# Moving weight scales, sums of squares and four weight sums from GpSimd to VectorE in a hybrid attention layer

## The chip, the cores and the metric

The kernel runs on one core of a Trainium2 chip. The core has a matrix engine (TensorE, PE in the profile), three engines for elementwise work (VectorE or DVE, ScalarE or ACT, GpSimd or POOL) and a sequencer (SyncE or SP) that here only issues DMAs. Each engine works through its own queue of instructions in order and waits on semaphores for the others; all DMAs share 16 DMA engines. Matmuls read SBUF and write PSUM banks of 512 float32 per partition. The metric is the device time of one execution in microseconds. A profile of one execution shows when each instruction ran and what it waited for.

## The reference

One encoder layer over 1024 tokens of width 1024, all in float32: an RMS norm, one input projection whose columns feed two kinds of attention (a sliding window and a 2-D neighbourhood), an output projection with a residual, a second RMS norm, a gated MLP of width 2816 whose gate passes a convolution of width 3, and a final RMS norm.

```python
hn = rmsnorm(h, norm_mix[l])
proj = jnp.einsum('bsd,de->bse', hn, w_in[l])
...                                   # o_a, o_b: the two attentions
mix = jnp.concatenate([rmsnorm(o_a, norm_a[l]), rmsnorm(o_b, norm_b[l])], axis=-1)
h = h + jnp.einsum('bse,ed->bsd', mix, w_out[l])
hn = rmsnorm(h, norm_ffn[l])
g = jnp.einsum('bsd,df->bsf', hn, w_gate); u = jnp.einsum('bsd,df->bsf', hn, w_up)
g = depthwise_conv3(g, conv_w) + conv_b
h = h + jnp.einsum('bsf,fd->bsd', jax.nn.silu(g) * u, w_down)
return rmsnorm(h, norm_final)
```

## The kernel before, in words

Tokens lie on the free axis in two halves of 512 (`h` = 0 and 1); features lie on the 128 partitions, so the width 1024 is 8 tiles `d` and the MLP width 2816 is 22 tiles `f`, called units. From the output projection on, float32 products are made of three 16-bit products: a weight and an operand are each split into an upper half (ScalarE copies to float16, `hi`, `whi`) and a lower half (VectorE subtracts, `lo`, `wlo`), and PE multiplies upper by upper, upper by lower and lower by upper. So every weight tile costs ScalarE one pass and VectorE one pass (L1062 for `wp`, L1089 for `wo`, L1141 for the rest) before PE can use it.

Weights are scaled into the range of float16 by a power of two. For a unit, ScalarE squares its gate and up weights with a running sum per row (`head_scan` L1054 into `head_rows` for the first four units, `scan_rows` L1154 into `w_rows` for the others, 24 more scans into `d_rows` for `w_down`). `settle_scales` (L1015) adds the gate and up sums (`wv`, L1021), and `measure` (L1006) takes their maximum over the partitions, by transposing on PE (`wm`, L1001) and reducing on VectorE (`m`, L1003), and then makes the scale: GpSimd clamps and multiplies (L1010) and raises to the power -1/2 (L1011), VectorE masks out all but the exponent (L240). Then come the inverse (`back`, L1024 and L1025) and the scaled taps of the convolution (`taps`, L1028). `settle_scales` runs twice for two of the first four units, during the output projection, and for four units at a time later on; `joint` (L1405 on) uses `measure` for the operands of the last product.

The stage around the change is the second part of the output projection (L1234 on). For each half `h` and each `d`, PE makes 12 matmuls into a bank `pj`; `settle_out` (L1184) adds the result to the residual on VectorE (`h<-pj`, L1188; the order lists call the eight tiles `h_4132`, `h_4249`, `h_4368`, `h_4494`, `h_4625`, `h_4703`, `h_4775`, `h_4777`), spills it by a DMA issued from ScalarE's queue, squares it on ScalarE (`s`, L1192) and adds the square to a running sum (`s<-s,s`, L1194): on GpSimd for the first half, on VectorE for the second. When a half is done, PE transposes the sum (`st`, L220), VectorE reduces it (`v`, L222 and L223), GpSimd raises it to -1/2 (L224), PE widens it over the partitions (`sw`, L255), VectorE multiplies `h` by it (`normed`, L1199), and `operands` splits it (`hg`, ScalarE L1172 and VectorE L1173).

In between, the first four units' weights are prepared. The MLP's products are formed by a scheme with seven products instead of eight, which takes sums and differences of weight blocks. `pure` splits two raw blocks of each unit (`wp<-rw`), and `head_weights` (L1204) forms `s1`, the sum of two blocks of the up weights (L1209, on GpSimd; tile `ws`), and then `s2`, `s4`, `s3` by subtractions on VectorE (L1201). The squares `s` and the sums `ws` share one set of six buffers of 512 columns, of which the four units' sums hold four.

PE's order is that of the program. On the other engines a scheduler sets it before the kernel runs: it takes instructions by priority and by its own estimate of when their inputs are ready; `high_priority` lifts some ahead. That order is then fixed, so an instruction that waits holds up all behind it on its engine. DMAs that load weights stand in SP's queue; a load into a buffer waits there until the buffer is free, and there are two buffers for scans.

Of the kernel before, what the change touches and what calls it, by code (L numbers as in the profile page):

```python
# [16 lines left out]
I32 = mybir.dt.int32  # L17
AF = mybir.ActivationFunctionType
ALU = mybir.AluOpType
# [36 lines left out]
C_END = 128  # L56
V_TOP, P_TOP, TINY = 2.0 ** 14, 2.0 ** 15, 1e-30
X_TOP, W_TOP, FAINT = 2.0 ** 7, 2.0 ** 13, 1e-24

K_ID, K_MA, K_MB, K_SCALE, K_END = 0, 128, 512, 896, 897  # L60


def hybrid_layer(tc, xT, w_in, w_out, w_gate, w_up, w_down, small, sink, rpb, consts, rope, out):
    nc = tc.nc
    with ExitStack() as ctx:
# [40 lines left out]
        minus_half = cpool.tile([128, 4], F32, name="minus_half")  # L106
# [120 lines left out]
        def inverse_narrow(sqs, dim, tag, n=4):  # L227

            ps = bank("ss", tag)
            for i, sq in enumerate(sqs):  # L230
                for c in range(n):
                    nc.tensor.matmul(ps[:, c:c + 1], sq[:, c * 128:(c + 1) * 128], ones[:, 0:1], start=c == 0 and i == 0,
                                     stop=i == len(sqs) - 1, skip_group_check=True)
            v = cpool.tile([128, 4], F32, name="v4", tag="v4", bufs=4)
            nc.scalar.activation(v[:, 0:n], ps[:, 0:n], AF.Sqrt, bias=eps, scale=float(D) / dim)
            nc.vector.reciprocal(v[:, 0:n], v[:, 0:n])
            return v

        def exponent(x):
            nc.vector.tensor_scalar(x.bitcast(I32), x.bitcast(I32), 0x7F800000, None, op0=ALU.bitwise_and)  # L240
# [478 lines left out]
        t = quarters(big("f", "mix"))  # L719
# [174 lines left out]
        for g in range(2):  # L894
            for b in range(NB):
                q, t, w = unit_window(g, b)
# [52 lines left out]
        for u in range(len(flat)):  # L949
            q, t, need, kind, _ = flat[u]  # L950
# [55 lines left out]
        def measure(v, tag):  # L1006

            with tc.high_priority(offset=500):
                s = spread_max(v, tag)
                nc.gpsimd.tensor_scalar(s, s, FAINT, W_TOP ** -2, op0=ALU.max, op1=ALU.mult)  # L1010
                nc.gpsimd.tensor_tensor(s, s, minus_half[:, 0:s.shape[1]], op=ALU.pow)  # L1011
                exponent(s)
            return s

        def settle_scales(i, n, tag):  # L1015

            fs = FO[i:i + n]
            n = len(fs)
            rows = (w_rows if i >= HEAD else head_rows)[:, 2 * i:2 * i + 2 * n].rearrange("p (n s) -> p n s", s=2)
            v = small("wv", 4)[:, 0:n]  # L1020
            nc.gpsimd.tensor_tensor(v, rows[:, :, 0], rows[:, :, 1], op=ALU.add)  # L1021
            s = measure(v, tag)
            back = little(4, "back", "backs", 4)[:, 0:n]
            nc.vector.reciprocal(back, s)  # L1024
            nc.gpsimd.tensor_tensor(back, back, unit_back.to_broadcast([128, n]), op=ALU.mult)  # L1025
            for j, f in enumerate(fs):
                taps = little(3, "taps", "taps", 12)
                nc.gpsimd.tensor_scalar(taps, par[:, C_CW + 3 * f:C_CW + 3 * f + 3], back[:, j:j + 1], 1.0, op0=ALU.mult, op1=ALU.mult)  # L1028
                scale_of[f], back_of[f], taps_of[f] = s[:, j:j + 1], back[:, j:j + 1], taps
# [67 lines left out]
        with behind("flip", "xr"):  # L1097
            for d in range(0, WO_EARLY, 2):
                t = big("wr", "op")[:, :].rearrange("p (d j c) -> p d j c", d=2, c=128)
# [9 lines left out]
        for h in range(2):  # L1109
            wide = widen(vb2[h], "pt")  # L1110
            for i in range(4):
                x = mix[4 + i][:, tsl(h)]
# [69 lines left out]
        late, total = [], [None, None]  # L1182
        at = lambda k, h: h1[k][:, tsl(h)]

        def settle_out():
            d, h, ps = late.pop(0)
            with tc.high_priority(offset=300):
                nc.vector.scalar_tensor_tensor(at(d, h), ps, wo_back, at(d, h), op0=ALU.mult, op1=ALU.add)  # L1188
            nc.scalar.dma_start(spilled[d][:, tsl(h)], at(d, h))
            s2 = half("s2")  # L1190
            with tc.high_priority(offset=300):
                nc.scalar.activation(s2, at(d, h), AF.Square)  # L1192
                if total[h] is not None:
                    (nc.gpsimd if d < (8, 0)[h] else nc.vector).tensor_tensor(s2, s2, total[h], op=ALU.add)  # L1194
            total[h] = s2

        def normed(h, wide, ds):
# [7 lines left out]
        def head_weights(i, name):  # L1205
            f, t = FO[i], wsum[i]
            g, u = head_raw[f]
            if name == "s1":
                nc.gpsimd.tensor_tensor(t, u[:, 0:4], u[:, 4:8], op=ALU.add)  # L1209
            elif name == "s2":  # L1210
                sub(t, t, g[:, 0:4])
            elif name == "s4":
                sub(t, g[:, 4:8], t)
            elif name == "s3":
                sub(t, g[:, 0:4], u[:, 0:4])
            else:
                t = u[:, 4:8]
            if name == "s1":
                if i % 2 == 0:
                    s1_places.extend(parts_places())  # L1220
                W[f, name] = two_parts(s1_places.pop(0), t, scale_of[f])
            else:
                W[f, name] = split_w(t, 4, scale_of[f])
# [4 lines left out]
        for d in range(WO_EARLY, KT):  # L1228
            if d % 2 == 0:
                t = fpool.tile([128, KT, 128], F32, name="raw", tag="raw", bufs=3)  # L1230
            wo_raw[d] = t[:, 4 * (d % 2):4 * (d % 2) + 4]
            nc.sync.dma_start(wo_raw[d], w_out[d, :, 4:8, :])
        for h in range(2):
            for d in range(KT):  # L1234
# [6 lines left out]
                if h == 1 and d == 1:  # L1241
                    with tc.high_priority(offset=300):
                        v = inverse_power(total[0], D, "pt")
# [612 lines left out]
```

## Time and profile before

| | |
|---|---|
| median of 3 runs | 1054.0 us (1052.48 to 1055.39) |
| the profiled execution | 1052.08 us, span 1050.3 us |
| PE busy | 1012.7 us, 96% |
| DVE busy | 886.0 us, 84% |
| ACT busy | 677.2 us, 64% |
| POOL busy | 247.2 us, 24% |
| GpSimd's power L1011, ten of them | 560 to 1262 ns |
| GpSimd's sums `ws` L1209, four of them | 1282 to 1796 ns |
| GpSimd's sums `s` L1194, seven of them | 1255 to 1723 ns |

Rows of the timeline read: start in us from the span's beginning, length in us of the group, engine, line, operation, tile written <- tiles read, shape, count, and in brackets the idle time of the engine just before it and what ended that. A group's length is the time from the start of its first to the end of its last instruction; neighbours on DVE overlap a little, since the next starts before the last has ended. Rows of waits read: who waited <- for whom, us in total, times, longest. Rows of groups give the shortest, median and longest in ns, and the first and last start.

### The profile page before, as it was taken

Reading aid. Unit: us, or ns where it says so; the run is one execution under the profiler, and the core shown is the slowest. Engines: PE = TensorE matmul, PEld = TensorE weight load, DVE = VectorE, ACT = ScalarE, POOL = GpSimd, SP = SyncE. Lnnn points to the kernel's source line nnn. Section 1 sums busy time; section 2 is a strip of 40 time slices with the busy share of each in tenths; the row PEclk is TensorE's granted clock in tenths of the full one; section 3 lists DMA queues with packets and bytes.
Section 4 is the critical chain, followed back from the end, with each engine's and each line's share of the span. In section 5 each row is a group of like instructions: output and inputs, shape, how many; then the busy total and the mean of one; then the engine's idle time right before and its main releaser. Section 6 shows DMA issues by size and latency. Waiting matters only on the chain.

```text
span 1050.3 us, 15578 instructions
## 1 busy us (share of the span) xinstructions
PE 1012.7 (96%) x5026; PEld 572.2 (54%) x5026; DVE 886.0 (84%) x1720; ACT 677.2 (64%) x1243; POOL 247.2 (24%) x379
## 2 busy tenths in 40 slices
PE   9998999999999977999999999999999999999996
PEld 7776777777775533444444444444444444444446
DVE  7699998766898789999899888888888889999874
ACT  8467787768687575778687875345454657655551
POOL 2235454676875344100101001001000000000002
PEclk9999999999999998999999999999999999999998
DMA  9437574686699743654767763332333678878744
GB/s 349 146 94 150 109 141 89 143 168 132 136 184 227 255 177 120 221 175 146 251 228 249 253 228 104 111 110 101 111 109 122 207 255 305 303 251 269 248 147 161
DMA packets 144274, 191.26 MB, mean 182 GB/s; under 512 B 77376, under 2 KB 88640, under 8 KB 144192
## 3 DMA queue, kind: packets, MB, share of 16 engines
q1 hardware_dynamic: 133536, 164.51, 54.9%
q10 hardware_dynamic: 10656, 25.76, 6.4%
q8 instruction: 39, 0.64, 0.3%
q14 instruction: 43, 0.35, 0.1%
HBM read 132.81 MB, written 28.57 MB: 154 GB/s over the span
## 4 chain that ended last, share of the span: by engine, by line
PE 60%; DVE 10%; ACT 4%; DMA 3%; issue 2%; POOL 1%; ACTq 0%; DVEq 0%; POOLq 0%
PE dn L1167 6%; PE dn L1165 6%; PE dn L1166 6%; PE z L1166 4%; PE z L1167 4%; PE z L1165 4%; PE pj L179 3%; PE y L1165 3%; PE y L1167 3%; PE y L1166 3%; PE x L1165 3%; PE x L1167 3%; PE x L1166 3%; PE pj L171 2%; PE pj L173 2%
## 5 line engine op out<-in xcount | busy, mean ns | idle before, releaser
L1167 PEld LDWEIGHTS <-wlo 128*128 128x128 f16 x898 | 87.8, 98 | 101.5 <-DVE wlo L1141 0.4
L1166 PEld LDWEIGHTS <-whi 128*128 128x128 f16 x898 | 87.8, 98 | 101.2 <-issue 0.9
L1165 PEld LDWEIGHTS <-whi 128*128 128x128 f16 x898 | 88.0, 98 | 100.2
L1167 PE MATMUL dn<-xd,wlo 128*128 128x512 f16 (+1 forms) x330 | 120.4, 365 | 0.0
L1166 PE MATMUL dn<-xd,whi 128*128 128x512 f16 (+1 forms) x330 | 120.4, 365 | 0.0
L1165 PE MATMUL dn<-xd,whi 128*128 128x512 f16 (+1 forms) x330 | 120.4, 365 | 0.0
L171 PE MATMUL pj<-xgh,whi 128*128 128x512 f32 x248 | 107.3, 433 | 0.6 <-ACT whi L155 0.6
L1167 PE MATMUL z<-hg,wlo 128*128 128x512 f16 x264 | 100.1, 379 | 0.0
L1165 PE MATMUL z<-hg,whi 128*128 128x512 f16 x264 | 100.1, 379 | 0.0
L1166 PE MATMUL z<-hg,whi 128*128 128x512 f16 x264 | 100.1, 379 | 0.0
L173 PE MATMUL pj<-xgh,wlo 128*128 128x512 f32 x248 | 98.3, 396 | 1.4 <-POOL wlo L156 1.4
L458 ACT ACTIVATE p<-p,nm 128x385 f32<-128x385 f32 (+3 forms) x128 | 74.7, 584 | 38.5 <-DVE nm L454 33.8
L172 PE MATMUL pj<-xgl,whi 128*128 128x512 f32 x248 | 97.9, 395 | 0.0
L1140 ACT ACTIVATE whi<-ws,m 128x512 f16<-128x512 f32 (+1 forms) x96 | 65.6, 708 | 33.2 <-DVE ws L1288 25.4
L1141 DVE SCALAR_TENSOR_TENSOR wlo<-ws,m,whi 128x512 f16<-128x512 f32 (+1 forms) x96 | 70.1, 739 | 13.2 <-ACT whi L1140 13.1
L1154 ACT ACTIVATE scan<-scan 128x1024 f32<-128x1024 f32 (+1 forms) x60 | 61.1, 1018 | 22.3 <-DMA scan<-in_w_down_dram 12.5
L1010 POOL TENSOR_SCALAR m<-m 128x4 f32<-128x4 f32 (+2 forms) x10 | 4.0, 404 | 256.1 <-DVE m L1003 255.9
L1141 DVE SCALAR_TENSOR_TENSOR wlo<-raw,m,whi 128x512 f16<-128x512 f32 (+1 forms) x78 | 55.1, 731 | 7.4 <-ACT whi L1140 6.7
L1165 PE MATMUL y<-hg,whi 128*128 128x512 f16 x160 | 60.6, 379 | 0.7 <-DVE c L1336 0.7
L1167 PE MATMUL y<-hg,wlo 128*128 128x512 f16 x160 | 60.6, 379 | 0.0
L1166 PE MATMUL y<-hg,whi 128*128 128x512 f16 x160 | 60.6, 379 | 0.0
L1140 ACT ACTIVATE whi<-raw,m 128x512 f16<-128x512 f32 (+1 forms) x78 | 51.5, 699 | 12.0 <-DMA raw<-in_w_down_dram 10.6
(290 smaller groups left out, 2490.1 us busy)
## 6 DMA issues: line engine op xcount, KB each, us to landing
xd<-x SPq DMA_DIRECT2D x77, 256.0 KB, 5.0
raw<-in_w_down_dram SPq DMA_DIRECT2D x64, 256.0 KB, 3.9
x<-c ACTq DMA_DIRECT2D x22, 512.0 KB, 2.9
scan<-in_w_gate_dram SPq DMA_DIRECT2D x18, 512.0 KB, 3.6
scan<-in_w_up_dram SPq DMA_DIRECT2D x18, 512.0 KB, 4.5
raw<-in_w_gate_dram SPq DMA_DIRECT2D x18, 512.0 KB, 3.5
raw<-in_w_up_dram SPq DMA_DIRECT2D x18, 512.0 KB, 3.8
raw<-in_w_in_dram SPq DMA_DIRECT2D x32, 256.0 KB, 3.2
```

Of the source, the lines that this page charges most:

```text
L171: nc.tensor.matmul(ps, w[0], x[0][:, tsl(h)], start=first, stop=False)
L172: nc.tensor.matmul(ps, w[0], x[1][:, tsl(h)], start=False, stop=False)
L173: nc.tensor.matmul(ps, w[1], x[0][:, tsl(h)], start=False, stop=last)
L179: nc.tensor.matmul(ps, a, b, start=i == 0 and b is x[h][0] and a is w[0], stop=i == len(ws) - 1 and a is w[1])
L458: nc.scalar.activation(p[:, 0:e], p[:, 0:e], AF.Exp, bias=nm, scale=-1.0, accum_out=sm)
L1010: nc.gpsimd.tensor_scalar(s, s, FAINT, W_TOP ** -2, op0=ALU.max, op1=ALU.mult)
L1140: nc.scalar.activation(hi, src, AF.Copy, scale=by)
L1141: nc.vector.scalar_tensor_tensor(lo, src, by, hi, op0=ALU.mult, op1=ALU.subtract)
L1154: nc.scalar.activation(t, t, AF.Square, accum_out=dst)
L1165: nc.tensor.matmul(ps, w[0], x[0], start=first and i == 0, stop=False, skip_group_check=True)
L1166: nc.tensor.matmul(ps, w[0], x[1], start=False, stop=False, skip_group_check=True)
L1167: nc.tensor.matmul(ps, w[1], x[0], start=False, stop=last and i == len(ws) - 1, skip_group_check=True)
```

## The change

Three things are different. First, the scale of a block is found on VectorE alone (`root_scale`): the float's bits are shifted right by one and masked, inverted and masked, and the result is multiplied by a constant, so that a power of two with half the negated exponent comes out; the clamp and the power on GpSimd are gone, and so is the mask `exponent` at this place. The scale can differ from the one before by a factor of two. Second, `wv` is added on VectorE. Third, all running sums of squares of the output projection and the four sums `s1` are added on VectorE. The power L224 of the norms stays on GpSimd, as do `back` and `taps`.

```diff
+W_ROOT = W_TOP * 2.0 ** 63
...
+        def root_scale(x):
+
+            i = x.bitcast(I32)
+            nc.vector.tensor_scalar(i, i, 1, 0x3FC00000, op0=ALU.logical_shift_right, op1=ALU.bitwise_and)
+            nc.vector.tensor_scalar(i, i, 0x3FC00000, 0x7F800000, op0=ALU.bitwise_xor, op1=ALU.bitwise_and)
+            nc.vector.tensor_scalar(x, x, W_ROOT, None, op0=ALU.mult)
...
             with tc.high_priority(offset=500):
                 s = spread_max(v, tag)
-                nc.gpsimd.tensor_scalar(s, s, FAINT, W_TOP ** -2, op0=ALU.max, op1=ALU.mult)
-                nc.gpsimd.tensor_tensor(s, s, minus_half[:, 0:s.shape[1]], op=ALU.pow)
-                exponent(s)
+                root_scale(s)
             return s
...
             v = small("wv", 4)[:, 0:n]
-            nc.gpsimd.tensor_tensor(v, rows[:, :, 0], rows[:, :, 1], op=ALU.add)
+            nc.vector.tensor_tensor(v, rows[:, :, 0], rows[:, :, 1], op=ALU.add)
...
                 if total[h] is not None:
-                    (nc.gpsimd if d < (8, 0)[h] else nc.vector).tensor_tensor(s2, s2, total[h], op=ALU.add)
+                    nc.vector.tensor_tensor(s2, s2, total[h], op=ALU.add)
...
             if name == "s1":
-                nc.gpsimd.tensor_tensor(t, u[:, 0:4], u[:, 4:8], op=ALU.add)
+                nc.vector.tensor_tensor(t, u[:, 0:4], u[:, 4:8], op=ALU.add)
```

The scheduler gives new orders to VectorE, ScalarE, GpSimd and SP; PE's order is the same. The rows below have each kernel's own line numbers; those of the changed kernel are 6 to 8 higher (L1188 is L1194 now, L1062 is L1068, L1089 is L1095, L1194 is L1200, L1209 is L1215).

VectorE from the first two scales on, before:

```order
L1188 SCALAR_TENSOR_TENSOR h_4249<-pj,wo_back,h_4249 128x512
L1003 TENSOR_REDUCE m<-wm 128x2
L1089 SCALAR_TENSOR_TENSOR wo<-wr,wo_by,wo 128x512
L240 TENSOR_SCALAR m<-m 128x2
L1089 SCALAR_TENSOR_TENSOR wo<-wr,wo_by,wo 128x512 x3
L1024 RECIPROCAL back<-m 128x2
```

and now:

```order
L1027 TENSOR_TENSOR wv<-head_rows 128x2
L1194 SCALAR_TENSOR_TENSOR h_4249<-pj,wo_back,h_4249 128x512
L1011 TENSOR_REDUCE m<-wm 128x2
L1095 SCALAR_TENSOR_TENSOR wo<-wr,wo_by,wo 128x512
L243 TENSOR_SCALAR m<-m 128x2
L1095 SCALAR_TENSOR_TENSOR wo<-wr,wo_by,wo 128x512
L244 TENSOR_SCALAR m<-m 128x2
L1200 TENSOR_TENSOR s_4993<-s_4993,s_4974 128x512
L245 TENSOR_SCALAR m<-m 128x2
L1095 SCALAR_TENSOR_TENSOR wo<-wr,wo_by,wo 128x512 x2
L1194 SCALAR_TENSOR_TENSOR h_4368<-pj,wo_back,h_4368 128x512
L1030 RECIPROCAL back<-m 128x2
```

The second `wv` stands ahead of `h_4249`, and the three bit steps and an `s` addition stand between the four `wo` halves.

VectorE ahead of tiles 6 and 7 of `wo` (`wo<-raw`), before:

```order
L240 TENSOR_SCALAR m<-m 128x2
L1062 SCALAR_TENSOR_TENSOR wp<-rw,m,wp 128x512
L1024 RECIPROCAL back<-m 128x2
L1188 SCALAR_TENSOR_TENSOR h_4625<-pj,wo_back,h_4625 128x512
L1062 SCALAR_TENSOR_TENSOR wp<-ws,m,wp 128x512
L1089 SCALAR_TENSOR_TENSOR wo<-raw,wo_by,wo 128x512 x2
```

and now:

```order
L243 TENSOR_SCALAR m<-m 128x2
L1068 SCALAR_TENSOR_TENSOR wp<-rw,m,wp 128x512
L244 TENSOR_SCALAR m<-m 128x2
L1068 SCALAR_TENSOR_TENSOR wp<-rw,m,wp 128x512
L245 TENSOR_SCALAR m<-m 128x2
L1200 TENSOR_TENSOR s_5061<-s_5061,s_5031 128x512
L1194 SCALAR_TENSOR_TENSOR h_4625<-pj,wo_back,h_4625 128x512
L1030 RECIPROCAL back<-m 128x2
L1215 TENSOR_TENSOR ws<-rw 128x512 x3
L1200 TENSOR_TENSOR s_5106<-s_5106,s_5061 128x512
L1194 SCALAR_TENSOR_TENSOR h_4703<-pj,wo_back,h_4703 128x512
L1095 SCALAR_TENSOR_TENSOR wo<-raw,wo_by,wo 128x512 x2
```

Two `s` additions, three `ws` sums and one more `h` now stand ahead of these halves, and the `wp<-ws` that stood there comes later; two more `s` additions stand ahead of it further up the queue.

VectorE around the reduction of the first half's sum (`v_5222`), before:

```order
L1201 TENSOR_TENSOR ws<-ws,rw 128x512 x2
L1188 SCALAR_TENSOR_TENSOR h_4132<-pj,wo_back,h_4132 128x512
L1141 SCALAR_TENSOR_TENSOR wlo<-ws,m,whi 128x512 x2
L1201 TENSOR_TENSOR ws<-ws,rw 128x512
L1188 SCALAR_TENSOR_TENSOR h_4249<-pj,wo_back,h_4249 128x512
L222 TENSOR_REDUCE v_5222<-st 128x4
L1141 SCALAR_TENSOR_TENSOR wlo<-ws,m,whi 128x512
L1194 TENSOR_TENSOR s_5228<-s_5228,s_5197 128x512
L223 TENSOR_SCALAR v_5222<-v_5222 128x4
L1141 SCALAR_TENSOR_TENSOR wlo<-ws,m,whi 128x512
```

and now:

```order
L1194 SCALAR_TENSOR_TENSOR h_4132<-pj,wo_back,h_4132 128x512
L1200 TENSOR_TENSOR s_5161<-s_5161,s_5140 128x512
L1207 TENSOR_TENSOR ws<-ws,rw 128x512
L1068 SCALAR_TENSOR_TENSOR wp<-ws,m,wp 128x512
L1200 TENSOR_TENSOR s_5179<-s_5179,s_5161 128x512
L1194 SCALAR_TENSOR_TENSOR h_4249<-pj,wo_back,h_4249 128x512
L223 TENSOR_REDUCE v_5222<-st 128x4
L1147 SCALAR_TENSOR_TENSOR wlo<-ws,m,whi 128x512
L1200 TENSOR_TENSOR s_5228<-s_5228,s_5197 128x512
L224 TENSOR_SCALAR v_5222<-v_5222 128x4
L1207 TENSOR_TENSOR ws<-ws,rw 128x512 x2
```

The last `s` addition of the first half (`s_5179`) stands on VectorE now, and the reduction follows `h_4249` as before, but with two halves `wlo` less ahead of it; behind it stand one `wlo` and one `s` addition, then two subtractions.

ScalarE at the same place as the `wo<-raw` rows, before:

```order
L1061 ACTIVATE wp<-rw,m 128x512 x2
L1192 ACTIVATE s_5061<-h_4494 128x512
L1189 DMA h1d<-h_4494 128x512
L1061 ACTIVATE wp<-ws,m 128x512
L1088 ACTIVATE wo<-raw,wo_by 128x512 x2
L1192 ACTIVATE s_5106<-h_4625 128x512
```

and now:

```order
L1067 ACTIVATE wp<-rw,m 128x512 x2
L1160 ACTIVATE scan,w_rows<-scan 128x1024
L1198 ACTIVATE s_5061<-h_4494 128x512
L1195 DMA h1d<-h_4494 128x512
L1160 ACTIVATE scan,w_rows<-scan 128x1024
L1195 DMA h1d<-h_4625 128x512
L1198 ACTIVATE s_5106<-h_4625 128x512
L1067 ACTIVATE wp<-ws,m 128x512
L1094 ACTIVATE wo<-raw,wo_by 128x512 x2
```

Two scans of later units' weights now stand ahead of the squares `s_5061` and `s_5106`.

## The prediction

> **What bounds the kernel.** I read the engines' shares first, then stretches of the span (each row: start and end, length, then the busy time and count of PE, PE's weight loads, DVE, ACT and POOL, PE's granted clock, DMA), then the waits, then single engines in order of time.
>
> ```profile
> PE 1012.7 (96%) x5026; PEld 572.2 (54%) x5026; DVE 886.0 (84%) x1720; ACT 677.2 (64%) x1243; POOL 247.2 (24%) x379
> ...
> 385.00:395.00 10.00, 6.66 (x32) 2.80 (x29) 7.85 (x12) 5.08 (x9) 9.03 (x11) 1.00 0.15 54
> 405.00:418.00 13.00, 8.26 (x35) 3.87 (x33) 12.04 (x17) 7.22 (x12) 4.13 (x3) 0.87 0.36 131
> 418.00:430.00 12.00, 12.00 (x57) 5.42 (x56) 12.00 (x20) 9.37 (x16) 0.00 (x0) 1.00 0.80 262
> 444.00:456.00 12.00, 12.00 (x50) 5.20 (x50) 10.20 (x16) 8.92 (x18) 0.00 (x0) 0.87 0.51 160
> 456.00:508.00 52.00, 52.00 (x244) 23.85 (x243) 47.77 (x72) 41.33 (x68) 3.63 (x8) 1.00 0.57 174
> ```
>
> TensorE (PE) is 96% busy, so a gain must come from where it is not: 385 to 395 (6.66 us of 10) and 405 to 418 (8.26 of 13), both in the output projection, where GpSimd (POOL) has its work. From 456 to 508 PE has no gap. The waits from 375 to 450 say who holds PE, and who holds VectorE (DVE):
>
> ```profile
> PE sw L255 <- POOL v L224: 4.5, 2, 2.4
> PE pj L179 <- DVE wo L1089: 4.0, 2, 3.8
> DVE m L240 <- POOL m L1011: 2.8, 2, 2.1
> PE st L220 <- POOL s L1194: 2.3, 1, 2.3
> ```
>
> So four PE starts count: the lower half of `wo` tile 6 (395.63), the transposed sums `st` (409.75), and the two widened norms `sw` (417.02 and 443.52).
>
> ```profile
> 395.63 11.79 PE L179 MATMUL pj<-mg,wo 128*128 128x512 f16 x46 [3.77 <-DVE wo L1089]
> 409.75 1.12 PE L220 MATMUL st<-cst,s 128*128 128x128 f32 x4 [2.33 <-POOL s L1194]
> 417.02 0.65 PE L255 MATMUL sw<-cst,v 128*128 128x128 f32 x4 [2.41 <-POOL v L224]
> 417.50 13.11 PE L179 MATMUL pj<-mg,wo 128*128 128x512 f16 x60
> 435.63 0.38 PE L1165 MATMUL x<-hg,wp 128*128 128x512 f16 x1
> 443.52 0.90 PE L255 MATMUL sw<-cst,v 128*128 128x128 f32 x4 [2.11 <-POOL v L224]
> 444.22 0.63 PE L1165 MATMUL x<-hg,wp 128*128 128x512 f16 x1
> ```
>
> **What the moved work costs on either engine.** DVE in that stage, then POOL, then two groups:
>
> ```profile
> 379.93 0.75 DVE L1089 SCALAR_TENSOR_TENSOR wo<-wr,wo_by,wo 128x512 f16<-128x512 f32 x1 [0.92 <-ACT wo L1088]
> 381.28 1.24 DVE L240 TENSOR_SCALAR m<-m 128x2 int32<-128x2 int32 x1 [0.60 <-POOL m L1011]
> 390.53 1.26 DVE L240 TENSOR_SCALAR m<-m 128x2 int32<-128x2 int32 x1 [2.15 <-POOL m L1011]
> 391.70 1.83 DVE L1062 SCALAR_TENSOR_TENSOR wp<-rw,m,wp 128x512 f16<-128x512 f32 x1
> 394.84 1.40 DVE L1089 SCALAR_TENSOR_TENSOR wo<-raw,wo_by,wo 128x512 f16<-128x512 f32 x2
> 399.54 3.46 DVE L1062 SCALAR_TENSOR_TENSOR wp<-rw,m,wp 128x512 f16<-128x512 f32 x2
> 404.90 1.75 DVE L1062 SCALAR_TENSOR_TENSOR wp<-ws,m,wp 128x512 f16<-128x512 f32 x1
> 407.89 2.35 DVE L1201 TENSOR_TENSOR ws<-ws,rw 128x512 f32<-128x512 f32 x2
> 413.42 0.68 DVE L222 TENSOR_REDUCE v<-st 128x4 f32<-128x512 f32 x1
> 417.70 1.41 DVE L1199 SCALAR_TENSOR_TENSOR h<-h,cst,sw 128x512 f32<-128x512 f32 x2 [0.96 <-PE sw L255]
> 433.84 2.49 DVE L1173 TENSOR_TENSOR hg<-h,hg 128x512 f16<-128x512 f32 x4
> ...
> 379.36 0.19 POOL L1021 TENSOR_TENSOR wv<-head_rows 128x2 f32<-128x2 f32 x1 [10.73 <-ACT junk L1054]
> 381.23 1.27 POOL L1194 TENSOR_TENSOR s<-s,s 128x512 f32<-128x512 f32 x1
> 408.11 1.58 POOL L1194 TENSOR_TENSOR s<-s,s 128x512 f32<-128x512 f32 x1 [2.01 <-ACT s L1192]
> 415.51 1.45 POOL L224 TENSOR_TENSOR v<-v,minus_half 128x4 f32<-128x4 f32 x1 [5.82 <-DVE v L223]
> 440.82 2.64 POOL L224 TENSOR_TENSOR v<-v,minus_half 128x4 f32<-128x4 f32 x1 [2.02 <-DVE v L223]
> ...
> L240 DVE TENSOR_SCALAR m<-m x10: 154/170/1258, 381.3 to 851.6; 128x4 int32<-128x4 int32 x4, 128x2 int32<-128x2 int32 x3, 128x1 int32<-128x1 int32 x3
> L1194 DVE TENSOR_TENSOR s<-s,s x7: 679/681/684, 414.7 to 433.2; 128x512 f32<-128x512 f32 x7
> ```
>
> A half such as `wo` at 394.84 takes DVE 0.74 us (two end in 1.40, so 0.66 from start to start). The same form takes 1.73 to 1.83 in five `wp` rows from 391.70 to 404.90, and the mask `m`, 0.17 at its median, takes 1.24 at 381.28, beside the POOL addition that began at 381.23. DVE thus already pays for POOL's additions. The excess is 1.1 each for the two `m`, 5.2 for the five `wp` rows, 1.1 for the pair at 407.89: 8.5 us, and 2.8 more are waited for POOL's `m`.
>
> Onto DVE come seven `s` and four `ws` additions, 0.68 each and 0.60 from start to start (as four `hg` in 2.49), 6.6 us; two more bit steps per scale, each between the 0.15 of the shortest `m` row and twice that, as it does two operations in one pass: taken as 0.15, 0.6 for the first two scales; two `wv` at about 0.1. DVE is relieved of 11.3 us and given 7.4.
>
> [...]
>
> **The sum, stage by stage**, by DVE's new order.
>
> 1. *To `wo` 6.* The second `wv` now stands in DVE's queue ahead of `h_4249`, and its input is ready at 379.36. Behind it wait `h_4249` (0.66) and the scale's reduction (0.3); the `wo` half of 379.93 starts at 380.45. From there to `wo` 6 DVE took 14.9 us. Of that go 0.60 + 1.1, 2.15 + 1.1, 1.1 of delay and one `wp` (0.66) that now comes later: 6.7. Four `s`, three `ws`, one `h` and four bit steps come: 2.4 + 1.8 + 0.66 + 0.6 = 5.5. So `wo` 6 starts at 380.45 + 13.7 = 394.1 instead of 394.84: gain 0.7.
> 2. *To `st`.* PE's 46 matmuls take 10.0 (0.218 each, as 60 in 13.11) to 11.8 us from 394.9: 404.9 to 406.7. On DVE the last `s` ends 18 rows behind `wo` 6, at 394.1 + 11.6 = 405.7, where POOL ended it at 409.7. I take 406.0: gain 3.75.
> 3. *To the first `sw`.* Before, 7.27 us, since DVE came to the reduction (413.42) 2.55 after `st` had ended. It now stands right behind `h_4249`: 0.9 (`st`) + 0.6 + one `wlo` 0.66 + one `s` 0.6 + 0.2 + the power that POOL keeps, between its rows' 1.45 and 2.64, taken midway as two DVE subtractions now run beside it, 2.05, + 0.1: 5.1. `sw` at 411.1: gain 5.9.
> 4. *To the first unit's second product* (435.63), which needs `hg_4625`, the first of the four at 433.84. That row stood 16.1 us and 25 DVE rows behind the norm at 417.70; it is 29 rows now, 2.6 us more: ready at 411.8 + 18.7 + 0.7 = 431.2. PE comes at 411.1 + 18.6 = 429.7 and waits 1.5 us, a new wait. Gain 4.4.
> 5. *To the second `sw`.* DVE does four `hg` and three `ws` first (430.5 + 2.4 + 1.8 = 434.7), then the reduction 0.6, one `wlo` 0.66, 0.23, the power at its own row's 2.64, 0.06: 438.9 instead of 443.52. Gain 4.6.
> 6. *The rest.* Eight later scales bring DVE some 0.4 us each for `wv` and bit steps and spare it POOL's chain. PE's unbroken matmuls hide both: nothing; uncovered, 3 us. POOL's `back` and `taps` stay.
>
> So 4.6 us off the profiled execution's 1052.08 (span 1050.3): 1047.5. That execution lies 1.9 below the median of the runs shown, 1054.0, so I forecast 1049.4. Under 0.3% (3.2 us) a difference can't be told from none.
>
> **Rivals.** (a) *The gain is lost again at 508.* The first later unit needs weights that come behind a scan:
>
> ```profile
> 505.77 1.06 ACT L1154 ACTIVATE scan<-scan 128x1024 f32<-128x1024 f32 x1 [1.48 <-DMA scan<-in_w_gate_dram]
> 506.83 1.32 ACT L1140 ACTIVATE whi<-raw,m 128x512 f16<-128x512 f32 x2
> 507.57 1.42 DVE L1141 SCALAR_TENSOR_TENSOR wlo<-raw,m,whi 128x512 f16<-128x512 f32 x2 [2.12 <-ACT whi L1140]
> ...
> L1165 PE MATMUL x<-hg,whi x8: 379/379/379, 508.3 to 518.1; 128*128 128x512 f16 x8
> ```
>
> PE uses them at 508.3, just as `wlo` ends. If the scans, paced by two buffers and their DMA, don't come earlier, `whi` stays at 506.83 and 1.5 to 4.6 us go back: 1051 to 1054. For it: the DMA wait in that row. Against: ACT's new order puts the first two scans ahead of `s_5061` and `s_5106`, near 387.
>
> (b) *Slower: `wv` stops DVE.* For later units `wv` stood in POOL's idle queue until ACT's scans had ended; on DVE all behind it waits. For the fourth of them the last two scans stand straight ahead of it on ACT, and the DMA can be late for them. Two stalls that reach PE with 3.8 us each (the longest that PE felt from DVE before) turn the 4.6 into 3.0 lost: 1057. It decides once the stalls exceed the 4.6 gained and what PE bridges from its open banks. Against: DVE's next halves wait for the same ACT queue already.
>
> (c) *More gain.* After the pause ahead of 444.22 the matmul takes 0.63 instead of 0.38, and the granted clock of 444 to 456 is 0.87, so about 13% of 12 us, 1.5, is lost there. If the new pauses don't bring the clock down, that goes too; with step 4's wait hidden (0.2 at the second `sw`, 1.5 at most) and 1.45 for both powers (1.2), 1045.2. [...]
>
> (d) *The excess isn't POOL's.* Then DVE gets 7.4 for the 2.8 of waits: 4.6 slower, 1058.6. Against it: from 418 to 430, where POOL is still, DVE does 20 rows in 12.00 us, 0.60 each.
>
> **Chances.** The forecast with its neighbours (1046.5 to 1050.5) 0.55, (c) 0.15, (a) 0.16, (b) 0.09, (d) 0.05: faster 0.70, same 0.16, slower 0.14. The range reaches from (c), 1045, to (a) whole with part of (b), 1056.
>
> **What the profile after would show.** Right: no `wp` or `m` row above 1 us from 380 to 412; `st` near 406; `sw` near 411 and 439; a PE wait of 1 to 2 us for `hg` near 430; none new after 456. Wrong: long `wp` rows without POOL (d); PE waiting for `wlo` between 500 and 508 (a); DVE waiting for scans between 530 and 630 with PE gaps (b).

## The result, and the profile after

| | kernel before | changed kernel |
|---|---|---|
| median on one chip, four runs each | 1054.7 us (1052.48 to 1056.46) | 1045.1 us (1044.44 to 1046.61) |
| ratio, 95% interval | | 0.9921 [0.9903, 0.9939] |
| profiled execution, and its span | 1052.08, 1050.3 | 1044.66, 1042.8 |

So the change gained 0.8%, 8.3 us by the ratio and 7.4 between the two profiled executions, where 4.6 was forecast. The profiles differ by 1.27 us already ahead of the changed code: the transposed sums of the norm before it begin at 360.58 before and at 359.31 after (why is shown behind long_pause). Places are therefore compared below from that row on.

The page of the changed kernel, engines' shares:

```profile
PE 1006.9 (97%) x5026; PEld 568.5 (55%) x5026; DVE 885.8 (85%) x1758; ACT 676.6 (65%) x1243; POOL 216.7 (21%) x341
```

DVE's busy time is where it was (886.0 before), with 38 instructions more. Stretches of the span around the change, of the kernel before and then of the changed one (columns as in the prediction):

```profile
376.00:415.00 39.00, 30.27 (x125) 12.92 (x123) 34.98 (x45) 21.88 (x35) 22.84 (x22) 0.91 0.31 116
415.00:460.00 45.00, 40.88 (x187) 18.94 (x188) 40.73 (x67) 35.75 (x67) 5.35 (x3) 0.96 0.64 200
```

```profile
376.00:415.00 39.00, 32.48 (x153) 14.57 (x151) 36.18 (x67) 30.13 (x52) 6.32 (x7) 1.00 0.57 197
415.00:460.00 45.00, 42.53 (x201) 19.57 (x200) 43.51 (x72) 36.10 (x68) 1.44 (x1) 1.00 0.62 195
```

In the same 39 us DVE now ends 67 instructions instead of 45 at hardly more busy time, so they are shorter on average; and PE's granted clock, 0.91 and 0.96 before, is 1.00. PE's rows in time, before (those that the prediction didn't show) and after:

```profile
380.74 4.92 PE L179 MATMUL pj<-mg,wo 128*128 128x512 f16 x22 [0.18 <-DVE wo L1089]
391.26 0.60 PE L179 MATMUL pj<-mg,wo 128*128 128x512 f16 x2 [0.20 <-ACT wo L1088]
410.66 3.94 PE L179 MATMUL pj<-mg,wo 128*128 128x512 f16 x12
```

```profile
378.75 0.61 PE L180 MATMUL pj<-mg,wo 128*128 128x512 f16 x2 [1.85 <-ACT wo L1094]
379.99 4.92 PE L180 MATMUL pj<-mg,wo 128*128 128x512 f16 x22 [0.63 <-DVE wo L1095]
391.48 0.61 PE L180 MATMUL pj<-mg,wo 128*128 128x512 f16 x2 [1.17 <-ACT wo L1094]
393.01 10.10 PE L180 MATMUL pj<-mg,wo 128*128 128x512 f16 x46 [0.92 <-DVE wo L1095]
404.05 0.63 PE L221 MATMUL st<-cst,s 128*128 128x128 f32 x4 [0.94 <-DVE s L1200]
404.51 2.75 PE L180 MATMUL pj<-mg,wo 128*128 128x512 f16 x12
408.27 0.65 PE L263 MATMUL sw<-cst,v 128*128 128x128 f32 x4 [1.00 <-POOL v L225]
428.82 0.38 PE L1172 MATMUL x<-hg,wp 128*128 128x512 f16 x1 [1.56 <-DVE hg L1179]
435.29 0.65 PE L263 MATMUL sw<-cst,v 128*128 128x128 f32 x4 [0.91 <-POOL v L225]
```

The same matmuls are shorter: 46 in 10.10 us where they took 11.79 at 395.63, 12 in 2.75 where they took 3.94. And most waits are shorter: 3.77 for `wo` is 0.92, 2.33 for the sum ahead of `st` is 0.94, 2.41 and 2.11 for the powers are 1.00 and 0.91. Two have grown, 0.18 to 0.63 and 0.20 to 1.17, both for earlier halves of `wo`, and one is new, 1.56 for `hg`. DVE and POOL of the changed kernel:

```profile
378.12 0.16 DVE L1027 TENSOR_TENSOR wv<-head_rows 128x2 f32<-128x2 f32 x1 [1.73 <-ACT junk L1060]
389.15 1.88 DVE L1215 TENSOR_TENSOR ws<-rw 128x512 f32<-128x512 f32 x3
392.20 1.41 DVE L1095 SCALAR_TENSOR_TENSOR wo<-raw,wo_by,wo 128x512 f16<-128x512 f32 x2
396.12 2.07 DVE L1068 SCALAR_TENSOR_TENSOR wp<-rw,m,wp 128x512 f16<-128x512 f32 x3
...
389.32 2.36 POOL L1031 TENSOR_TENSOR back<-back,cst 128x2 f32<-128x2 f32 x1 [3.57 <-DVE back L1030]
406.83 1.38 POOL L225 TENSOR_TENSOR v<-v,minus_half 128x4 f32<-128x4 f32 x1 [14.53 <-DVE v L224]
433.80 1.44 POOL L225 TENSOR_TENSOR v<-v,minus_half 128x4 f32<-128x4 f32 x1 [25.59 <-DVE v L224]
```

Three `wp` halves take 2.07 together, where one alone had taken 1.83; no `wp` or `m` row is above 1 us any more. POOL is held up as well: its `back` of two columns, begun beside DVE's three `ws` additions, takes 2.36, where it took 0.19 at 384.65 in the kernel before.

The gain splits in two. From the earlier norm's `st` to the first `y` of the first unit's products the kernel before needs 95.47 us (360.58 to 456.05) and the changed one 86.83 (359.31 to 446.14). Take PE's waits out, 14.91 and 11.11, and 80.56 and 75.72 are left for the very same matmuls. So 3.8 us came from shorter waits and 4.8 from the clock. The clock's part in detail, half microseconds of the kernel before:

```profile
395.50:396.00 0.50, 0.37 (x2) 0.21 (x3) 0.50 (x2) 0.50 (x2) 0.50 (x2) 0.99 0.90 340
396.00:396.50 0.50, 0.50 (x3) 0.15 (x1) 0.50 (x2) 0.50 (x2) 0.50 (x1) 0.50 0.50 184
...
399.00:399.50 0.50, 0.50 (x3) 0.16 (x2) 0.50 (x1) 0.50 (x2) 0.42 (x2) 0.60 0.02 8
```

The clock falls to 0.50 at 395.99 (0.99 in the first row) and is back at 399.40 (0.60 in the last: 0.40 at half). Done so for all half microseconds from 360 to 460, the kernel before has three such drops, 395.99 to 399.40, 409.64 to 413.06 and 443.78 to 447.19, each 3.41 us long, each costing up to 1.7 (half of it, at half clock); the changed kernel has none.

Behind `y` 2.4 us of the 8.64 are given back in this profile: 1.3 by the first later unit (up to 500.15), of which 0.9 come back soon behind it, and 2.05 in the last product (828.55 to 1008.77, 180.22 us, where it took 178.17). What is left, 6.2, and the 1.27 from ahead are the 7.5 between the spans.

### The profile page after: what moved, and what is told of

It reads as the page before. It is cut to its first block, busy times and chain, and to the rows that moved or that the text cites. A ratio compares the mean times of both kernels' runs of the same rounds, so it can differ in the third digit from the quotient of the medians.

```text
span 1042.8 us, 15570 instructions
## 1 busy us (share of the span) xinstructions
PE 1006.9 (97%) x5026; PEld 568.5 (55%) x5026; DVE 885.8 (85%) x1758; ACT 676.6 (65%) x1243; POOL 216.7 (21%) x341
## 4 chain that ended last, share of the span: by engine, by line
PE 43%; DVE 22%; DMA 9%; issue 4%; ACT 3%; SPq 1%; POOL 0%; DVEq 0%; ACTq 0%; POOLq 0%
PE z L1172 4%; PE z L1173 4%; PE z L1171 4%; DMA xd<-x 4%; PE x L1173 3%; PE x L1172 3%; PE x L1171 3%; PE y L1173 3%; DVE wlo L1147 3%; PE y L1172 3%; PE y L1171 3%; DVE xd L1555 3%; DMA raw<-in_w_down_dram 2%; PE pj L180 2%; PE pj L172 2%
## 5 line engine op out<-in xcount | busy, mean ns | idle before, releaser
L1031 POOL TENSOR_TENSOR back<-back,cst 128x4 f32<-128x4 f32 (+1 forms) x7 | 4.3, 620 | 354.8 <-DVE back L1030 335.3
L1555 DVE SCALAR_TENSOR_TENSOR xd<-xd,m 128x512 f16<-128x512 f32 x77 | 55.0, 747 | 6.4 <-ACT xd L1554 6.4
```

Of the source, the lines that this page charges most:

```text
L1555: nc.vector.scalar_tensor_tensor(lo, t[:, HALF:S], by, hi, op0=ALU.mult, op1=ALU.subtract)
```

## The experiments

Two theories at first. A: POOL's 512-wide additions hold up DVE's instructions beside them, so moving them is the gain. B: the wait is for POOL's results, the chain of the scale above all. Four kernels do parts of the change; all are timed against the kernel before on one chip (median 1052.26).

**scales_only**: only the bit steps for the scale; `wv`, `s` and `ws` stay on POOL.

```diff
-                nc.gpsimd.tensor_scalar(s, s, FAINT, W_TOP ** -2, op0=ALU.max, op1=ALU.mult)
-                nc.gpsimd.tensor_tensor(s, s, minus_half[:, 0:s.shape[1]], op=ALU.pow)
-                exponent(s)
+                root_scale(s)
```

> Only the scales by bit steps on VectorE; wv, the running sums s and the four sums ws stay on GpSimd. Theory A (GpSimd's 512-wide additions hold VectorE up, and that is the main cost): 1 to 3 us below before, from the 2.8 us of waits for GpSimd's m; wp rows of 1.7 us and more stay. Theory B (the latency of the scale's chain through GpSimd is the main cost): 6 to 8 us below before.

1050.23, ratio 0.9979 [0.9964, 0.9995]. **s_only** moves the running sums alone (the first pair of lines), **ws_only** the four additions for `s1` (the second), **sums_only** both; the scale's chain and `wv` stay on POOL:

```diff
-                    (nc.gpsimd if d < (8, 0)[h] else nc.vector).tensor_tensor(s2, s2, total[h], op=ALU.add)
+                    nc.vector.tensor_tensor(s2, s2, total[h], op=ALU.add)
...
-                nc.gpsimd.tensor_tensor(t, u[:, 0:4], u[:, 4:8], op=ALU.add)
+                nc.vector.tensor_tensor(t, u[:, 0:4], u[:, 4:8], op=ALU.add)
```

> Only s and ws on VectorE; the scales (clamp, power, mask) and wv stay on GpSimd. Theory A: 5 to 7 us below before, no wp row above 1 us, st some 4 us earlier. Theory B: within 2 us of before, since VectorE has 6.6 us more to do and still waits for GpSimd's m.

> Only the seven running sums s of the first half on VectorE. Theory A: about two thirds of what sums_only gains, 3 to 5 us, by seven of eleven additions, and long wp rows only beside the four ws additions. Theory B: within 1 us of before.

> Only the four sums ws on VectorE. Theory A: about a third of what sums_only gains, 1 to 3 us. Theory B: within 1 us of before.

sums_only 1046.44, ratio 0.9944 [0.9923, 0.9966]; s_only 1047.02, 0.9949 [0.9930, 0.9967]; ws_only 1045.61, 0.9938 [0.9918, 0.9958]. What DVE's rows from 376 to 414 us take above the length that the same shape has in the changed kernel (the excess), and PE's wait for the sum ahead of `st`:

- the kernel before has 9.0 us of excess (the prediction's rows, 8.5, and two smaller ones) and waits 2.33 us;
- scales_only 10.0 and 3.99: DVE saves its waits for POOL's `m`, but PE waits longer for POOL's `s`;
- s_only 2.5 and 0.63; ws_only 5.2 and 3.21; sums_only none and 0.81.

Of scales_only, PE ahead of `st` and DVE:

```profile
407.37 0.66 PE L221 MATMUL st<-cst,s 128*128 128x128 f32 x4 [3.99 <-POOL s L1200]
...
386.70 1.24 DVE L243 TENSOR_SCALAR m<-m 128x2 int32<-128x2 int32 x1
387.85 1.84 DVE L1068 SCALAR_TENSOR_TENSOR wp<-rw,m,wp 128x512 f16<-128x512 f32 x1
```

So B falls: with the chain of the scale wholly on DVE most of the gain is missing, and with it wholly on POOL most of it is there. But A's split fell too: in time the two groups don't add up. Either alone gives about what both give, and the intervals can't rank them. The table further down shows why.

**dummy_add**: is it POOL's work, or who waits for its results? Eleven additions go back to POOL, seven in `settle_out` and four in `head_weights`, and nobody reads them.

```diff
+                    if h == 0:
+                        nc.gpsimd.tensor_tensor(idle, at(d, 0), at(d, 0), op=ALU.add)
...
+                nc.gpsimd.tensor_tensor(idle, at(2 * i, 0), at(2 * i, 0), op=ALU.add)
```

> The changed kernel, with eleven 128x512 additions put back on POOL that nothing reads (seven beside the sums of the first half, four beside the sums for s1), so that POOL's work is there again and nobody waits for it. Theory A (a POOL addition of two 128x512 inputs holds up VectorE's instructions beside it, whoever needs its result): rows of VectorE of over 1 us between 376 and 414 us come back, with an excess of 5 to 11 us; the first sw comes 3 to 6 us later than in the changed kernel (408.3), and the time is 1048 to 1052, ratio 0.995 to 0.999. Theory B (the time went into waits for POOL's results): excess 0 to 1 us, first sw within 1 us of the changed kernel's, ratio 0.992.

1052.03, ratio 1.0004 [0.9990, 1.0017]: the whole gain is gone, more than A had expected, with PE, DVE and ACT in the same order as in the changed kernel. DVE, then POOL, then PE of this kernel:

```profile
390.16 1.00 DVE L244 TENSOR_SCALAR m<-m 128x2 int32<-128x2 int32 x1
391.74 1.00 DVE L245 TENSOR_SCALAR m<-m 128x2 f32<-128x2 f32 x1
393.25 0.74 DVE L1194 SCALAR_TENSOR_TENSOR h<-pj,wo_back,h 128x512 f32<-128x512 f32 x1
396.75 1.52 DVE L1200 TENSOR_TENSOR s<-s,s 128x512 f32<-128x512 f32 x1
...
379.29 1.04 POOL L1202 TENSOR_TENSOR idle<-h 128x512 f32<-128x512 f32 x1 [15.03 <-ACT wo L1094]
389.59 1.54 POOL L1202 TENSOR_TENSOR idle<-h 128x512 f32<-128x512 f32 x1 [0.70 <-DVE m L243]
391.21 3.02 POOL L1219 TENSOR_TENSOR idle<-h 128x512 f32<-128x512 f32 x2
...
380.93 6.61 PE L180 MATMUL pj<-mg,wo 128*128 128x512 f16 x22 [1.36 <-DVE wo L1095]
396.31 1.04 PE L180 MATMUL pj<-mg,wo 128*128 128x512 f16 x2 [3.36 <-ACT wo L1094]
399.65 12.87 PE L180 MATMUL pj<-mg,wo 128*128 128x512 f16 x46 [2.31 <-DVE wo L1095]
```

DVE's excess from 376 to 414 is 8.1 us again. From the earlier `st` to `y` this kernel is 10.1 us behind the changed one, 5.2 of them in PE's waits and 4.9 by the clock (the table below). An `m` of two columns takes 1.00 beside a POOL addition instead of 0.16, and ends as the addition does (391.16 and 391.13). An `s` with both inputs in SBUF takes 1.52 instead of 0.68; `h<-pj`, with one input in PSUM, begins at 393.25 amid POOL's pair and takes its usual 0.74. POOL pays as well: the addition at 379.29, which begins ahead of the DVE row that it holds up, takes 1.04, the next ones 1.54 and, two together, 3.02.

**dummy_set**: the control. In the same eleven places POOL reads one column and then fills the tile.

```diff
+                nc.gpsimd.tensor_copy(idle[:, 0:1], at(2 * i, 0)[:, 0:1])
+                nc.gpsimd.memset(idle, 0.0)
```

> The same, but in each of the eleven places POOL reads one column of the tile (128x1) and then writes a whole 128x512 tile with a constant: as many POOL writes, at the same places, with hardly anything read. If it is POOL's reading of two inputs that blocks VectorE, no rows of VectorE over 1 us between 376 and 414 beyond the changed kernel's, and the changed kernel's time within 1 us (ratio 0.991 to 0.993). If any POOL instruction on wide tiles holds VectorE up, an excess of 4 us or more and 1048 to 1051.

1046.1, ratio 0.9944 [0.9928, 0.9960]: by the ratio 2.4 us above the changed kernel, where at most 1 was expected (the intervals overlap), and no DVE row is longer. DVE, POOL and PE:

```profile
399.36 0.75 DVE L1194 SCALAR_TENSOR_TENSOR h<-pj,wo_back,h 128x512 f32<-128x512 f32 x1 [2.12 <-POOL idle L1220]
...
390.31 0.52 POOL L1221 MEMSET idle<- 128x512 f32 x1
390.89 2.48 POOL L1220 COPY idle<-h 128x1 f32<-128x1 f32 x1
...
380.15 6.58 PE L180 MATMUL pj<-mg,wo 128*128 128x512 f16 x22 [0.63 <-DVE wo L1095]
407.96 1.09 PE L221 MATMUL st<-cst,s 128*128 128x128 f32 x4 [3.15 <-DVE s L1200]
```

So POOL's filling of whole tiles, 0.52 us each, cost DVE nothing here, and additions that read whole tiles did: 8.1 us of excess against none. The 2.4 us are the control's own: DVE once waits 2.12 until POOL has read an `h` tile that it is to overwrite (POOL's one-column copy was itself held for 2.48 beside DVE's `ws` additions), and PE's clock drops twice, though the waits of 1.85 and 0.63 ahead of the first drop are those of the changed kernel, which has none there.

That last point made a third question: what decides a drop? Finding all drops from half microseconds as above:

| kernel | `st` to `y` | PE's waits in it | rest | drops (start) | ratio |
|---|---|---|---|---|---|
| before | 95.47 | 14.91 | 80.56 | 395.99, 409.64, 443.78 | |
| scales_only | 95.81 | 15.37 | 80.44 | 408.69, 415.51, 442.82 | 0.9979 |
| s_only | 89.33 | 13.54 | 75.79 | none | 0.9949 |
| ws_only | 88.47 | 12.55 | 75.92 | none | 0.9938 |
| sums_only | 89.28 | 11.89 | 77.39 | 394.72 | 0.9944 |
| changed | 86.83 | 11.11 | 75.72 | none | 0.9921 |
| after_second | 86.82 | 11.11 | 75.71 | none | 0.9925 |
| long_pause | 88.17 | 12.45 | 75.72 | none | 0.9937 |
| dummy_add | 96.93 | 16.33 | 80.60 | 381.40, 395.05 (10.24 long) | 1.0004 |
| dummy_set | 91.03 | 12.20 | 78.83 | 380.13, 407.44 | 0.9944 |
| after_wv_pool | 87.84 | 10.52 | 77.32 | 393.20 | 0.9905 |
| late_scans | 88.24 | 9.90 | 78.34 | 373.11 (6.83 long) | 0.9917 |
| early_norm | 84.98 | 8.88 | 76.10 | none | 0.9895 |

The rest is 75.7 to 76.1 without a drop, and 1.2 to 1.7 us more for each 3.41 us at half clock. By the waits alone the parts come nearer to adding up: s_only saves 1.4, ws_only 2.4, sums_only 3.0, the whole change 3.8. Every drop lasts 3.41 us or two or three times that. And within one execution all drops start at the same point of a grid of 3.413 us: in the kernel before 409.64 and 443.78 lie 13.65 and 47.79 behind 395.99, that is 4.00 and 14.00 steps; in scales_only 6.82 and 34.13, 2.00 and 10.00 steps; in dummy_set 27.31, 8.00. Between executions the grid lies differently: the drops of sums_only and after_wv_pool begin 1.27 and 2.79 us ahead of 395.99, no whole step. A stretch of 3.41 us between two points of an execution's grid is called a window here, and such a point a border; in the changed kernel, without a drop, the clock's fall at the end, behind PE's last matmuls, gives the grid (1036.46). In the window ahead of a drop PE stood still for 3.05, 2.2 and 2.1 us in the kernel before, 2.07 in sums_only, 2.0 in after_wv_pool (a pause of 1.17 and 0.82 of the next one), 1.95 in late_scans. In the kernel before the pause of 2.41 ahead of 417.02 lies across a border, 1.86 on the near side, and no drop follows; nor does one behind 1.90 in one window of scales_only (401.86 to 405.28). An estimate from these numbers, for this case: a drop comes when PE is idle for more than some 1.8 to 2 of 3.41 us, and the pauses of one window add up. The two pauses of dummy_set above fall into one window almost whole (2.45 us from 376.72); in the changed kernel a border, at 377.69, cuts them, and the fuller window has 1.69.

**after_second, long_pause**: the changed kernel again, and with the pause ahead of the second `sw` made longer by a second power, to the exponent 1, in the second half's norm alone.

```diff
             nc.gpsimd.tensor_tensor(v, v, minus_half, op=ALU.pow)
+            if again:
+                nc.gpsimd.tensor_tensor(v, v, plain, op=ALU.pow)
...
-            v = inverse_power(total[1], D, "pt")
+            v = inverse_power(total[1], D, "pt", again=True)
```

> The changed kernel again, unchanged. Theory A': where PE's clock drops is a matter of when its pauses fall, not of the kernel: a pause of 1 to 2 us costs a further 1.6 to 1.7 us in some executions and nothing in others. Then this profile may show a stretch of 22 or 46 matmuls that is 1.6 to 1.7 us longer than in the first profile of the same kernel (4.92 and 10.10) at the same waits, and the time is 1043 to 1046 by the chip (ratio 0.990 to 0.994). Theory B' (the clock answers to the length of the pauses): the same waits, no stretch longer than in the first profile.

> The changed kernel with a second power on POOL, to the exponent 1, behind the one of the second half, so that only the pause ahead of the second sw grows: from 0.91 us to about 2.35 (the power's 1.44), as long as that of the kernel before (2.11). By the length of the pause alone (B') PE's clock drops behind it as it did before: the 48 matmuls up to y take 11.8 to 12.1 instead of 10.4, time 1047.5 to 1048.5 (ratio 0.995). If the drop is a matter of when the pause falls (A'): at least the pause, 1.4 us, and up to 1.7 more, 1046.5 to 1048 (ratio 0.994 to 0.995), with 10.4 or 12.0 in the profile.

after_second 1043.97, ratio 0.9925 [0.9907, 0.9943]: same waits, no drop, 86.82 from `st` to `y`. It doesn't tell the theories apart by itself. long_pause 1045.70, ratio 0.9937 [0.9920, 0.9954], 1.7 above after_second on the same chip (the intervals overlap):

```profile
437.00 0.65 PE L267 MATMUL sw<-cst,v 128*128 128x128 f32 x4 [2.25 <-POOL v L229]
```

The pause grew from 0.92 to 2.25, longer than the 2.11 behind which the clock fell in the kernel before, and no drop followed: `y` begins 10.85 us behind this row, as it does in the changed kernel (435.29 to 446.14). So the length alone (B') doesn't decide it; nor did a drop follow the pause of 3.21 ahead of `st` in ws_only or that of 2.91 ahead of the first `sw` in s_only. That a border cut these pauses is an estimate by the windows above: where the grid lies in an execution without a drop from 360 to 460 is shown for the changed kernel alone.

The stretch from 57 to 63 us, far ahead of the change, shows the same with nothing changed at all. PE's instructions up to the earlier norm are the same in both kernels, and here each has two pauses, 0.64 (before) or 0.70 (changed) and then 1.36 us, some 0.7 us apart. The matmul behind the second, of the kernel before and of the changed one:

```profile
61.27 0.63 PE L173 MATMUL pj<-xgh,wlo 128*128 128x512 f32 x1 [1.36 <-POOL wlo L156]
61.67 0.50 PE L174 MATMUL pj<-xgh,wlo 128*128 128x512 f32 x1 [1.36 <-POOL wlo L157]
```

In the kernel before both, 2.00 us, lie in one window (58.07 to 61.48), and the clock drops at 61.48 for 3.41 us (the next three matmuls take 0.63 us each, 0.40 in the changed kernel). In the changed kernel a border divides them, at 60.25, so that no window has more than 1.36, and it doesn't. The earlier norm's `st` begins at 360.58 and 359.31; in the other profiles it lies near the one or the other, at 360.14 to 361.00 in four (s_only, after_wv_pool, late_scans, early_norm) and at 358.86 to 359.68 in seven. So, by an estimate from these, most of the 1.27 us by which the changed kernel's profile is ahead at `st` is this drop, and chance.

How far single profiles are typical can be read from the granted clock of every timed run. By the arithmetic above one drop takes half of 3.41 us, some 0.0016 of the span's mean clock. The 45 runs of the kernel before that stand beside the experiments have 0.988 to 0.993, 0.9912 on average; the changed kernel's ten (with after_second) have 0.994 to 0.998, 0.9963 on average. That is an estimate of three drops fewer per execution, as in the stretch of the two profiles. So the clock's part of the gain isn't the luck of two executions; and the changed kernel does have drops in some, since 0.994 is about two drops below the 0.997 of its profiled executions.

**after_wv_pool**: the changed kernel with `wv` back on POOL.

```diff
-            nc.vector.tensor_tensor(v, rows[:, :, 0], rows[:, :, 1], op=ALU.add)
+            nc.gpsimd.tensor_tensor(v, rows[:, :, 0], rows[:, :, 1], op=ALU.add)
```

> The changed kernel with one of its parts undone: the sums of the two rows (wv, 128x2) are back on POOL. The changed kernel's VectorE waits 1.73 us at 378 us for ScalarE's last scan, and PE 0.63 us right after for the lower half of wo. If that wait is on the path, the PE wait of 0.63 goes and the first st comes 0.5 to 1.5 us earlier against the start of the section; time 1044.0 to 1045.0 (ratio 0.991 to 0.992). If it is hidden, 1045 to 1046, with the wait turned into one of VectorE for POOL.

1041.73, ratio 0.9905 [0.9887, 0.9923], against the changed kernel's 0.9921 and 0.9925 not told apart by the interval. PE:

```profile
380.29 4.92 PE L180 MATMUL pj<-mg,wo 128*128 128x512 f16 x22 [0.18 <-DVE wo L1095]
393.31 11.72 PE L180 MATMUL pj<-mg,wo 128*128 128x512 f16 x46 [0.93 <-DVE wo L1095]
```

The wait of 0.63 is 0.18: `wv` on DVE costs 0.45 there. In this execution a drop ate it (46 matmuls in 11.72), behind waits of 1.17 and 0.93 that are the changed kernel's own.

**late_scans**: in addition ScalarE's scans of units 2 and 3 are written behind the product's second group.

```diff
-        for i in range(HEAD):
+        for i in range(2):
             for j in range(2):
                 head_scan(i, j)
...
+                if h == 0 and d == 1:
+                    for i in range(2, HEAD):
+                        for j in range(2):
+                            head_scan(i, j)
```

> after_wv_pool, and in addition ScalarE's scans of units 2 and 3 are written behind the second group of the product, so that ScalarE makes wo of groups 2 and 3 ahead of the last scans. In the changed kernel PE waits 1.85 us at 379 for ScalarE's wo, and 0.63 for VectorE's. If these waits are lost time for good, both go and the time is 2 to 2.5 us below the changed kernel: 1042.5 to 1043 (ratio 0.990). If later waits (sums of squares, the later wo) give the time back, st comes as late as before and the time stays at 1045.

1043.47, ratio 0.9917 [0.9900, 0.9934], so no gain over after_wv_pool on the same chip. The wait of 1.85 for ScalarE's `wo` is gone, but it returned:

```profile
371.29 0.38 PE L180 MATMUL pj<-mg,wo 128*128 128x512 f16 x1 [0.51 <-ACT mg L1121]
374.21 7.94 PE L180 MATMUL pj<-mg,wo 128*128 128x512 f16 x23 [2.54 <-DVE mg L1122]
```

ScalarE, now making `wo` ahead of the first operands `mg`, is late for these, and PE's waits fall by 0.6 us only (10.52 to 9.90). The expected 2 us weren't lost time for good.

**early_norm**: after_wv_pool, with the norm of the first half's upper four tiles written one tile earlier.

```diff
-                if h == 1 and d == 4:
+                if h == 1 and d == 3:
                     normed(0, wide, K2)
```

> The changed kernel with wv back on POOL and the norm of the first half's upper four tiles written one tile earlier, so that VectorE makes hg ahead of two additions (ws) and a lower half (wlo). In the changed kernel PE waits 1.56 us for hg at 428.8; on VectorE about 1.3 to 2 us of work now stands behind hg. If VectorE's order is what PE waits for, the wait falls to 0.5 us or less, the second sw comes 1 us or more earlier against the first, and the time is 1 to 1.5 us below that of the changed kernel with wv on POOL (ratio 0.989 to 0.990). If the second norm's chain takes the time back, the pause ahead of the second sw grows from 0.91 by as much, and the time stays (0.9905).

1042.04, ratio 0.9895 [0.9876, 0.9914]; on the same chip its six runs (1039.40 to 1042.77) all lie below those of after_second (1042.79 to 1046.46).

```profile
428.71 0.38 PE L1172 MATMUL x<-hg,wp 128*128 128x512 f16 x1 [0.29 <-DVE hg L1179]
430.52 0.38 PE L1172 MATMUL x<-hg,wp 128*128 128x512 f16 x1 [0.35 <-DVE hg L1179]
435.13 0.65 PE L263 MATMUL sw<-cst,v 128*128 128x128 f32 x4 [0.34 <-POOL v L225]
```

The wait for `hg` falls from 1.56 to 0.64 and the next one from 0.91 to 0.34. It is faster than the changed kernel, and has the lowest ratio of all that ran; from after_wv_pool (0.9905) the intervals don't tell it apart.

## Why the prediction was right, and where it was not

Measured from the earlier norm's `st`, so without the 1.27 us from ahead of the change:

| step of the prediction | gain forecast | gain measured |
|---|---|---|
| 1, `wo` 6 | 0.7 | 1.35 |
| 2, `st` | 3.75 | 4.43 |
| 3, first `sw` | 5.9 | 7.48 |
| 4, the first unit's second product (435.85 before, 428.82 after) | 4.4 | 5.76 |
| 5, second `sw` | 4.6 | 6.96 |
| `y` (not in the sum) | | 8.64 |
| 6, end of the span | 4.6 | 6.23 |

- **The mechanism** was right. The excess of 8.5 us that the prediction read off the long DVE rows is what dummy_add brings back, 8.1, and it takes the whole gain with it. Rival (d), that the excess isn't POOL's, is out.
- **Step 1**: `wv` does stop DVE, 1.73 us for the last scan, and PE pays 0.45 of it. The rest went better than counted: `wo` 6 came 0.65 earlier than forecast.
- **Step 2**: the 46 matmuls took 10.10, the low end of the 10.0 to 11.8 that the step allowed, since no drop came. DVE's last `s`, not PE, then set `st`, with a wait of 0.94, as the step had it.
- **Steps 3 and 5**: the power on POOL is the term that was mis-sized. It was taken at 2.05 and 2.64 and measured 1.38 and 1.44, though DVE had two additions beside the first. So 0.7 and 1.2 us more were gained. The row of 2.64 in the kernel before was no price of the power alone: it lasted longer beside DVE's rows, as DVE's do beside POOL's. DVE's rows beside it:

```profile
440.65 0.74 DVE L1141 SCALAR_TENSOR_TENSOR wlo<-ws,m,whi 128x512 f16<-128x512 f32 x1
441.31 0.69 DVE L1301 TENSOR_TENSOR ws<-raw 128x512 f32<-128x512 f32 x1
441.92 0.68 DVE L1201 TENSOR_TENSOR ws<-rw 128x512 f32<-128x512 f32 x1
```

  The power ends at 443.46, 0.86 us behind the third; in the changed kernel it ends at 435.24, 0.86 behind the first of two `wlo` rows (433.63, 0.75 long). The powers of the first half end 0.87 behind a `wlo` row in the kernel before (at 416.96) and 0.88 behind a `ws` subtraction in the changed one (at 408.21), rows with two inputs in SBUF as well; one that begins beside an `h<-pj` alone, at 364.31 in the kernel before, takes 1.00. Why the power ended behind the first row here and behind the third there, no run shows.
- **Step 4**: a new wait of 1.5 for `hg` was forecast; it is 1.56, and early_norm shows that it was DVE's order.
- **Step 6** was wrong: where it took "nothing", 2.4 us were given back. Rival (a) came true in small, 0.63 for ScalarE's `whi` at 499.17 and 0.37 for DVE's `wlo`. In the last product PE waits 1.0 and 1.7 us for `whi` and `wlo` in the changed kernel's two profiles, but not at all in long_pause, whose instructions stand there in the same order, nor in after_wv_pool and early_norm. So it isn't the order alone; what else it takes stays open.
- **The clock** is the larger miss. The sum left it out, and rival (c) gave it 1.5 us; it was 4.8, more than the waits' 3.8. The prediction looked for the drop only behind the last pause, where a matmul of 0.63 showed it, and used the drop of 395.63's row (11.79) as the end of a range instead of asking what would become of it. (c) was nearest in its time, 1045.2, but not in its detail: the wait for `hg` did come.
- **The size** is in part luck. The gain of 8.3 us is nearly twice the 4.6 of the sum, and 1045.1 lies at the lower edge of the range, 1045, which (c) had set. The clock and the powers gave more than was counted, and the end took 2.4 back.
- **Rival (b)**: no PE gap behind a scan from 530 to 630. The 0.60 from start to start that the prediction took for each moved addition is borne out: three `ws` take 1.88.

## What to carry to other kernels

An engine that looked idle wasn't free to use here: beside GpSimd's additions, which read two inputs in SBUF, VectorE's rows with both inputs in SBUF grew to about twice their length (a `wp` half from 0.74 to between 1.73 and 1.84 us, an `s` from 0.68 to 1.52), and GpSimd's own rows grew too (an addition from 1.04 to 1.54). The excess over the usual length shows before the move what VectorE pays; how much of it reaches TensorE is another matter, here 3.8 us of waits for 9.0 of excess. Where PE pauses, count each pause twice, once as a wait and once as a share of a window, here of 3.41 us; pauses that together filled more than some 1.8 to 2 us of one cost up to 1.7 us more here, so several small pauses that are cut below that are worth more than their sum. Judge variants by waits and clock apart, and the clock over many runs, since a single profile shows one position of the grid.

## What the runs showed that was not expected

- PE's clock drops in units of 3.41 us on a grid that runs through the whole execution (in the kernel before 288.00 steps from 61.48 to 1044.52, where the clock falls at the end) and lies differently in each (table above); the same waits of 1.85 and 0.63 were followed by 4.92 us for 22 matmuls in the changed kernel and by 6.58 in dummy_set, and two like pauses near 60 us by a drop in the kernel before and by none in the changed one.
- The blocking reaches tiny instructions on both sides: DVE's `m` of 128x2 with one input takes 1.00 to 1.26 us instead of 0.16 beside a POOL addition, and, beside three DVE additions, POOL's copy of one column 2.48, where two others take 0.64 and 0.75, and its `back` 2.36 instead of 0.20.
- The power of the norms on POOL, 1.38 to 2.64 us long beside DVE's rows with two inputs in SBUF, ends 0.86 to 0.88 us behind one of them, and takes 1.00 where only an `h<-pj` stands beside its start (364.31, before).
